# Hymba block on one core: state-space units on a closer pace, the mixing stage's start moved, Newton roots on GpSimd

## The chip, the cores and the metric

One core of one Trainium2 chip runs the whole layer in a single launch. The metric is the device time in microseconds, the median of three runs. Engines are named as in the profile: PE (TensorE) with its weight loads PEld, DVE (VectorE), ACT (ScalarE), POOL (GpSimd), and SP, whose queue issues most of the DMAs.

## The reference

A pre-normalised input (2048 tokens, width 1024) is projected once. Its columns feed a diagonal state-space layer (32 groups of 16 channels, 64 complex states each) and a chunked attention with 8 heads. Both outputs are normalised, joined, and projected back; then comes a SwiGLU feed-forward part and a last normalisation.

```python
h = rmsnorm(x, norm_mix_g)
proj = h @ w_in                       # u_ssm, q, k, v: 512 columns each
# state space: scan over time, y = Re(C s) + D u, then
y = gelu(y); y_ssm = y * sigmoid(y @ w_glu + b_glu)
y_att = chunked_attention(q, k, v, rel_bias)   # own chunk of 64 and 8 before
mixed = concat([rmsnorm(y_ssm, g_ssm), rmsnorm(y_att, g_att)])
x = x + mixed @ w_out
h2 = rmsnorm(x, norm_ffn_g)
x = x + (silu(h2 @ w_gate) * (h2 @ w_up)) @ w_down
out = rmsnorm(x, norm_final_g)
```

## The kernel before

Every large product is done in three matmuls of a reduced-precision float type: `split` makes a high part (a cast on ACT) and a low part (a subtraction on DVE), and `mm3` adds high x high, high x low and low x high. Tokens lie along the free dimension in four blocks of 512.

The stages follow each other:

- `u_phase` projects the state-space input and works out the state-space constants.
- `att_phase` runs attention in 128 steps (`scores`, then `transp` two steps later, then `pv_head` and `pv_scale`), one step for 128 queries of one head. Between the steps it advances units of other work: the projections of q, k and v (`qk_unit`, `v_unit`), the normalised inputs (`hT_unit`) and eight state-space units (`ssm_unit`). Each `Unit` has a first and a last step, and `advance` spreads its yields evenly over them. State-space unit b runs from step `2 + int(SW * b)` to `2 + int(SW * (b + 1))`.
- `mix_phase` is a generator too. At step `OPEN` = 119 the attention's input buffers are released and it is opened: it loads the gate's weights (`load_wg`, four tiles `sg` through two buffers). From step `GSTART` it is advanced to step 130: it loads the first block of state-space outputs (`load`: four DMAs into `yr`, one GELU into `ys`, splits into `gh` and `gl`) and of attention outputs (`load_a`), yields `PY` times, then runs the gate's matmuls (`glu`, 16 yields, with the norm's sums at yield `RA1` and the spread of its roots at `RA2`), and yields `PZ` times. The rest of the stage runs after the last step: the gate of the second block, `split_wo` for the eight tiles of `w_out`, then `w_out` block by block.
- `gate_up_phase` and `down_phase` are the feed-forward part.

A state-space unit loads its inputs through SP (`U`, `Bst`, `Tm`, `Vm`; `U` has one buffer), multiplies them (`pj<-U,Bst`), copies the result to `X` on ACT, scans it on POOL (L601 to L613), moves the states to `XG` by DMA (L635), forms the output (`pj<-U,Tm` and `pj<-XG,Vm`), and stores it (`y<-X`, L648).

`newton` turns a mean square into a reciprocal root: an integer seed, then three Newton steps, all on tiles of 128x4. It is called by `rstd1` in the mixing stage, by `rstd_steps` for the later norms, and by `u_phase`. `spread` then transposes the roots across partitions on PE.

The order of the instructions on an engine is the planner's: it orders by its own costs and by priority, except that PE's matmuls, and whatever else is passed to `keep_in_program_order`, keep the order of the program. DMAs of one queue are issued in order.

Of the kernel before, what the change touches and what calls it, by code (L numbers as in the profile page):

```python
# [11 lines left out]
I32 = mybir.dt.int32  # L12
AF = mybir.ActivationFunctionType
ALU = mybir.AluOpType
AX = mybir.AxisListType

P = 128
SEQ, D = 2048, 1024
KT = D // P
DS = 512  # L20
# [11 lines left out]
EPS = 1e-6  # L32
LAG = 2
NSMALL = 100
WB = 3
OPEN, GSTART = 119, 122
R1 = 13
SGB = 2
RA1, RA2 = 2, 12
# [7 lines left out]
LPH = 2  # L47
V0 = 0, 4
DB, XB = 3, 2
SW = 15  # L50
CUT = -8, -2, 2, 7, 13, 19, 24
CUTL = -8, -2, 2, 7, 13, 19, 23
ORDER = "sptf"
# [43 lines left out]
def f32(ap):  # L97
    return ap.bitcast(F32)


def newton(k, pool, ps, n, w):

    V = k.nc.vector
    v, f, y, o = (k.t(pool, t, [P, w], bufs=2) for t in ("nv", "nf", "ny", "no"))
    V.tensor_scalar(v[:], ps, 1.0 / n, EPS, op0=ALU.mult, op1=ALU.add)
    V.tensor_copy(f[:], v[:].bitcast(I32))
    V.tensor_scalar(f[:], f[:], -0.5, 1597463007.0, op0=ALU.mult, op1=ALU.add)
    V.tensor_copy(y[:].bitcast(I32), f[:])
    V.tensor_scalar(v[:], v[:], -0.5, None, op0=ALU.mult)
    for a, b in ((y, o), (o, y), (y, o)):  # L110
        V.tensor_tensor(f[:], a[:], a[:], op=ALU.mult)
        V.tensor_tensor(f[:], f[:], v[:], op=ALU.mult)
        V.scalar_tensor_tensor(b[:], f[:], 1.5, a[:], op0=ALU.add, op1=ALU.mult)
    return o


def tok_sums(k, te, ps, c, sq):

    for i in range(4):
        te.matmul(ps[:, c + i : c + i + 1], sq[:, i * P : (i + 1) * P], k.ones[:], start=True, stop=True)  # L120
# [5 lines left out]
        te.transpose(pb[:, i * P : (i + 1) * P], o[:, c + i : c + i + 1].to_broadcast([P, P]), k.ident[:])  # L126


def rstd_steps(k, te, psum, pool, tag, sq, n, out, **kw):

    nt = out.shape[-1] // P
    ps = k.t(psum, *tag, **kw)
    sqs = sq if isinstance(sq, list) else [sq]
    for i in range(nt):
        for m, sq in enumerate(sqs):
            te.matmul(ps[:, i : i + 1], sq[:, i * P : (i + 1) * P], k.ones[:], start=m == 0, stop=m == len(sqs) - 1)
    with k.tc.high_priority():
        o = newton(k, pool, ps[:, :nt], n, nt)
    yield
    pb = k.t(psum, *tag, **kw)  # L140
    for i in range(nt):
        te.transpose(pb[:, i * P : (i + 1) * P], o[:, i : i + 1].to_broadcast([P, P]), k.ident[:])
    k.nc.scalar.copy(out, pb[:, : nt * P])
    yield
# [8 lines left out]
def split(k, hi, lo, raw):  # L153
    nc = k.nc
    return nc.scalar.copy(hi, raw), nc.vector.tensor_tensor(lo, raw, f32(hi), op=ALU.subtract)  # L155
# [244 lines left out]
def u_phase(k, ident, S, aw):  # L400
# [3 lines left out]
    with ExitStack() as cx:  # L404
# [54 lines left out]
        def sums(b):  # L459
            with tc.high_priority():  # L460
                ST[b] = newton(k, p2 if b else aw, ST[b][:], D, 4)
# [215 lines left out]
def att_phase(k, ident, S, aw, x0, roots):  # L677

    tc, nc, io, pfs = k.tc, k.nc, k.io, k.pfs
    with ExitStack() as cx:  # L680
# [256 lines left out]
        for b in range(NG // GB):  # L937
            units.append(Unit(ssm_unit(k, sp, psum, S, b, k.ssm_eng), SSM_N, 2 + int(SW * b), 2 + int(SW * (b + 1)), light=SL))
        N = len(steps)
# [19 lines left out]
        yield mix  # L959


PY, PZ = 8, 1
MIX_N = 17 + PY + PZ


def mix_phase(k, S, bank):

    tc, nc, io = k.tc, k.nc, k.io
    te = k.te
    with ExitStack() as cx:  # L970
        rx = ExitStack()
        my = rx.enter_context(tc.tile_pool(name="my", reuse_waits="tile", bufs=1, side="right"))
        mz = rx.enter_context(tc.tile_pool(name="mz", reuse_waits="tile", bufs=1, side="right"))
# [5 lines left out]
        W, Wg = {}, {}  # L979
# [8 lines left out]
        def load_wo(n, pool, tag, **kw):  # L988
            raw = k.t(pool, tag, [P, 1024], **kw)
            nc.sync.dma_start(raw[:], io["w_out"][QS[n] * P : (QS[n] + 1) * P, :])  # L990
            return raw

        def split_wo(raws):
            for n, q in enumerate(QS):
                W[q] = k.t(mx, f"woh{q}", [P, D], F32R), k.t(mx, f"wol{q}", [P, D], F32R)
                raw = raws[n] if n < len(raws) else load_wo(n, wr, "xt")
                split(k, W[q][0][:], W[q][1][:], raw[:])

        def squares(src):
            sq = k.t(mz, "sq", [P, SB], bufs=2)  # L1000
# [14 lines left out]
        def load(sb, one=False):  # L1015
            b = B()
            b.o = {}
            yt = k.t(my, "ys", [P, 4, SB], bufs=2)
            b.ys, b.g = [yt[:, f] for f in range(4)], []
            if sb % 2 == 0:  # L1020
                yrs[0] = k.t(my, "yr", [P, 4, L, 128])
                for f in range(4):
                    nc.sync.dma_start(yrs[0][:, f], S["y"][f * P : (f + 1) * P, :, sb * 64 : sb * 64 + 128])
            yv = b.yr = yrs[0][:, :, :, (sb % 2) * 64 : (sb % 2 + 1) * 64]
            fs = [slice(0, 4)] if one else [slice(f, f + 1) for f in range(4)]
            for s in fs:
                nc.scalar.activation(yt[:, s].rearrange("p f (c j) -> p f c j", j=L), yv[:, s].rearrange("p f j c -> p f c j"), AF.Gelu_apprx_tanh)  # L1027
            for f in range(4):
                gh, gl = k.t(my, f"gh{f}", [P, SB], F32R), k.t(my, f"gl{f}", [P, SB], F32R)
                split(k, gh[:], gl[:], b.ys[f])  # L1030
                b.g.append((gh, gl))
            return b
# [33 lines left out]
        def rstd1(b, c, ps):  # L1066

            tok_sums(k, te, ps, 0, b.sqs if c else b.sqa)
            with tc.high_priority():
                b.o[c] = newton(k, mz, ps[:, :4], DS, 4)  # L1070

        def rstd2(b, c, pb):

# [3 lines left out]
        def big():  # L1077
            return k.t(psum, *BIG)

        def norm(b, n):  # L1080
            ps = big()
            pcs = [ps[:, 512 * c : 512 * c + 512] for c in range(2)]
            if n:
                for c in range(2):
                    spread(k, te, pcs[c], b.o[c], 0)
            for c in range(2):
                (rstd2 if n else rstd1)(b, c, pcs[c])
# [53 lines left out]
        b = load(0, True)  # L1141
# [4 lines left out]
        for n, _ in enumerate(glu(b, bank, True)):  # L1146
            if n == RA1:
                rstd1(b, 0, bank())
            if n == RA2:
                pb = bank()  # L1150
                spread(k, te, pb, b.o[0], 0)
                rstd2(b, 0, pb[:])
            yield
# [9 lines left out]
        for n, _ in enumerate(glu(nxt, bk, True)):  # L1163
            if n == R1:
                rstd1(b, 1, bk())
            yield
        psum, mx = k.psum, k.mx
        raws += [load_wo(n, mx, f"m{QS[n + 2]}") for n in range(2, 6)]
        b.m = {}
        mixed(b, 0)  # L1170
        split_wo(raws)
        load_a(nxt, 1)
        xr = pre = None
        for sb in range(NSB):
# [3 lines left out]
            if sb == 0:  # L1178
                held = [w_out(0, b, 2 * n) for n in range(2)]
                next(held[0])  # L1180
                ps = big()
# [27 lines left out]
            if sb < NSB - 1:  # L1209
                xr = rstd_steps(k, te, psum, k.mf, BIG, b.sa[:], D, S["rsn"][:, sb * SB : (sb + 1) * SB])  # L1210
# [3 lines left out]
            b = nxt  # L1214
# [121 lines left out]
def gate_up_phase(k, S):  # L1336
# [3 lines left out]
    with ExitStack() as cx:  # L1340
# [6 lines left out]
        def bank(n):  # L1347
            return k.t(psum[n], n, [P, 512])

        xr = rstd_steps(k, te, psum["X"], k.mf, ("X", [P, 512]), k.last, D, S["rsn"][:, (NSB - 1) * SB :])  # L1350

        raws = cycle((k.gr,) * 2 + (g2,) * 2)
# [121 lines left out]
def down_phase(k, S):  # L1474
    tc, nc, io = k.tc, k.nc, k.io
    V, te = nc.vector, k.te
    with ExitStack() as cx:
        fa = cx.enter_context(tc.tile_pool(name="fa", reuse_waits="tile", bufs=1))
        a0, r1, r2, a1 = (cx.enter_context(tc.tile_pool(name=n, reuse_waits="tile", bufs=b, side="right")) for n, b in (("a0", 1), ("r1", 4), ("r2", 6), ("a1", 1)))
        ring = cycle((r1,) * 4 + (r2,) * 6)  # L1480
        dx, dy = (cx.enter_context(tc.tile_pool(name=n, bufs=4, space=bass.MemoryType.PSUM, reuse_waits="tile")) for n in ("dx", "dy"))
# [50 lines left out]
        class End:  # L1532
# [15 lines left out]

            def sums(self):
                self.rs = k.t(fa, "rs", [P, 512])  # L1550
                self.r = rstd_steps(k, k.te, dy, fa, ("ps", [P, 512]), self.sa, D, self.rs[:, : self.n])
                next(self.r)

            def products(self):
# [144 lines left out]
```

## Time and profile before

| | us |
|---|---|
| median of 3 runs | 2292.94 (2292.49 to 2293.21) |
| the profiled execution's own time | 2291.46 |
| its span, first to last instruction | 2289.7 |
| PE busy | 2176.4 (95%) |
| DVE busy | 1544.3 (67%) |
| ACT busy | 1000.6 (44%) |
| POOL busy | 350.4 (15%) |

The mean granted clock of TensorE over the span is 0.976. Attention and the state-space units lie between about 125 and 740 us, the mixing stage's products end near 976, the gate and up products near 1820, and the down products run to the end. POOL works until about 683 us; behind that its row in the page is empty.

How the views are read: a row of the timeline gives the start, the duration, the engine, the line of the kernel, and the tiles written and read; in brackets stands how long the engine was idle before it and what ended that idle time. A row of SPq is the issue of a DMA. A row of the table of stretches gives a stretch's length and the busy time of PE, PEld, DVE, ACT and POOL in it (with instruction counts), the granted clock, the share of DMA time and the rate.

### The profile page before, as it was taken

How to read it: one execution, taken by the hardware profiler on the slowest of the kernel's cores; microseconds unless marked ns; L12 is line 12 of the kernel's file. 1: busy time of each engine (PE TensorE's matmuls, PEld its weight loads, DVE VectorE, ACT ScalarE, POOL GpSimd, SP SyncE). 2: the span in 40 equal slices, each digit the busy share in tenths (PEclk: the TensorE clock that was granted, in tenths of full speed). 3: DMA queues.
4: the chain of work that ended last, by engine and by line, in shares of the span. 5: the costliest groups of instructions: out<-in, count | busy, mean ns of one | idle time of the engine just before them, and what ended most of it. 6: DMA issues, size and time to landing. Idle time of an engine off the chain costs nothing.

```text
span 2289.7 us, 30275 instructions
## 1 busy us (share of the span) xinstructions
PE 2176.4 (95%) x10632; PEld 1833.7 (80%) x10632; DVE 1544.3 (67%) x2695; ACT 1000.6 (44%) x1655; POOL 350.4 (15%) x813
## 2 busy tenths in 40 slices
PE   8988899999997899999999999999999999999997
PEld 6777688898986688878888887888888778888886
DVE  7745565556556756776767678667666477688776
ACT  6444555455557552343333335333333343353321
POOL 2245765455660000000000000000000000000000
PEclk9998999999998899999999999999999999999998
DMA  8667786676643534854555467555333286465642
GB/s 299 229 224 221 257 219 205 188 199 172 191 133 116 170 124 153 274 180 143 180 179 202 160 204 266 186 173 198 129 97 111 99 326 240 167 231 181 221 161 74
DMA packets 215256, 428.33 MB, mean 187 GB/s; under 512 B 38592, under 2 KB 61168, under 8 KB 208000
## 3 DMA queue, kind: packets, MB, share of 16 engines
q1 hardware_dynamic: 210368, 412.50, 55.2%
q0 software_dynamic: 4736, 13.91, 2.0%
q8 instruction: 83, 1.36, 0.2%
q14 instruction: 69, 0.57, 0.1%
HBM read 286.86 MB, written 129.00 MB: 182 GB/s over the span
## 4 chain that ended last, share of the span: by engine, by line
PE 83%; DVE 4%; DMA 3%; issue 2%; ACT 2%; POOL 2%; SPq 1%; DVEq 0%; POOLq 0%; ACTq 0%
PE X L79 20%; PE ps L79 20%; PE Y L79 10%; PE pf L79 9%; PE big L79 9%; PE W L79 5%; PE pj L79 4%; PE sc L79 2%; PE pt L82 2%; SPq L563 1%; SPq L648 0%; POOL X L604 0%; DVE ptl L867 0%; ACT ys L1027 0%; DMA lo<-hc 0%
## 5 line engine op out<-in xcount | busy, mean ns | idle before, releaser
L79 PE MATMUL X<-hi,c 128*128 128x512 f32 x1408 | 451.2, 391 | 6.7 <-DVE c L155 5.4
L79 PE MATMUL ps<-hd,hd 128*128 128x512 f32 (+1 forms) x1968 | 432.9, 382 | 5.7 <-DVE hd L155 3.3
L79 PEld LDWEIGHTS ps<-hd,hd 128*128 128x128 f32 x1968 | 359.8, 190 | 77.4 <-DVE hd L155 4.4
L79 PEld LDWEIGHTS X<-hi,c 128*128 128x128 f32 x1408 | 265.6, 189 | 63.2 <-DVE c L155 6.3
L79 PE MATMUL X<-lo,c 128*128 128x512 f32 x704 | 275.1, 391 | 0.0
L155 ACT CAST hd<-hd 128x1536 fp32r<-128x1536 f32 (+1 forms) x106 | 147.6, 1393 | 238.0 <-DMA hd<-hq 189.0
L79 PE MATMUL Y<-hi,c 128*128 128x512 f32 x704 | 224.3, 389 | 1.5 <-DVE u L1388 1.5
L155 DVE TENSOR_TENSOR hd<-hd 128x1536 fp32r<-128x1536 f32 (+1 forms) x106 | 174.1, 1644 | 28.7 <-ACT hd L155 28.1
L155 DVE TENSOR_TENSOR c<-S,c 128x512 fp32r<-128x512 f32 x176 | 120.9, 688 | 97.0 <-ACT c L155 96.7
L1512 DVE TENSOR_TENSOR acc<-acc,ps 128x512 f32<-128x512 f32 x196 | 131.3, 684 | 52.3 <-PE ps L79 50.8
L1384 ACT COPY u<-X 128x512 f32<-128x512 f32 x132 | 77.4, 587 | 200.0 <-PE X L79 200.0
L79 PE MATMUL big<-m,woh 128*128 128x512 f32 x512 | 163.1, 400 | 0.0
L79 PE MATMUL pf<-hi,w 128*128 128x512 f32 x416 | 153.8, 422 | 8.5 <-ACT w L155 4.7
L155 ACT CAST c<-S 128x512 fp32r<-128x512 f32 x176 | 109.5, 622 | 119.3 <-PE Y L79 61.6
L79 PEld LDWEIGHTS Y<-hi,c 128*128 128x128 f32 x704 | 132.2, 188 | 29.7 <-DVE u L1388 2.2
L79 PEld LDWEIGHTS X<-lo,c 128*128 128x128 f32 x704 | 132.8, 189 | 27.7
L155 ACT CAST c<-raw 128x512 fp32r<-128x512 f32 x132 | 82.2, 623 | 151.9 <-PE Y L79 68.5
L79 PE MATMUL Y<-lo,c 128*128 128x512 f32 x352 | 137.0, 389 | 0.0
L867 DVE TENSOR_TENSOR ptl<-pt,pth 128x640 fp32r<-128x640 f32 (+3 forms) x152 | 98.3, 647 | 46.7 <-ACT pth L866 45.1
L851 ACT ACTIVATE s<-s,mn 128x640 f32<-128x640 f32 (+4 forms) x128 | 98.0, 765 | 65.4 <-DVE mn L848 60.7
L866 ACT CAST pth<-pt 128x640 fp32r<-128x640 f32 (+3 forms) x152 | 83.8, 551 | 92.0 <-PE pt L82 87.9
L79 PE MATMUL W<-hi,c 128*128 128x512 f32 x352 | 115.5, 389 | 0.0
(440 smaller groups left out, 4174.5 us busy)
## 6 DMA issues: line engine op xcount, KB each, us to landing
w<-wss SPq DMA_DIRECT2D x36, 1024.0 KB, 6.0
hq<-g SPq DMA_DIRECT2D x140, 256.0 KB, 2.1
hd<-hq SPq DMA_DIRECT2D x42, 768.0 KB, 4.5
hd<-wc SPq DMA_DIRECT2D x42, 768.0 KB, 6.0
raw<-in_w_gate SPq DMA_DIRECT2D x44, 512.0 KB, 3.7
raw<-in_w_up SPq DMA_DIRECT2D x44, 512.0 KB, 4.3
wc<-px SPq DMA_DIRECT2D x66, 256.0 KB, 3.2
wss<-w SPq DMA_DIRECT2D x12, 1024.0 KB, 5.6
```

The lines of the kernel that those rows point to most:

```text
L79: return self.tc.keep_in_program_order(self.tc.nc.tensor.matmul(*a, **b))
L82: return self.tc.keep_in_program_order(self.tc.nc.tensor.transpose(*a, **b))
L155: return nc.scalar.copy(hi, raw), nc.vector.tensor_tensor(lo, raw, f32(hi), op=ALU.subtract)
L563: ins = nc.sync.dma_start(out, in_)
L851: nc.scalar.activation(s[:, :nk], s[:, :nk], AF.Exp, bias=mn[:], scale=-1.0, accum_out=sums[sb, pr][:, hh, qp : qp + 1])
L866: nc.scalar.copy(pth[:, a:b, qp, :], pt[:, a:b, :])
L867: nc.vector.tensor_tensor(ptl[:, a:b, qp, :], pt[:, a:b, :], f32(pth[:, a:b, qp, :]), op=ALU.subtract)
L1384: nc.scalar.copy(u[:], ps[:])
L1512: V.tensor_tensor(a, a, ps[:], op=ALU.add)
```

## The change

- `SW` goes from 15 to 14.25: the eight state-space units start at steps 2, 16, 30, 44, 59, 73, 87 and 101 and the last ends at 116 (before: 2, 17, 32, 47, 62, 77, 92, 107, and 122).
- `GSTART` goes from 122 to 120 and `PY` from 8 to 11. `MIX_N` grows by three with it. The state-space buffers are released at step 120.
- `newton` makes its seed in one operation on integers in place of three. With `aside`, only the mean stays on DVE (kept in program order) and the remaining 14 operations go to POOL, where the fused third operation of a Newton step is two. `aside` holds for `rstd1` and for `rstd_steps` except at the tail; `u_phase` and the tail stay on DVE with 12 operations.
- The low halves of `split_wo` are kept in program order on DVE.

```diff
-OPEN, GSTART = 119, 122
+OPEN, GSTART = 119, 120
...
-SW = 15
+SW = 14.25
...
-def newton(k, pool, ps, n, w):
+def newton(k, pool, ps, n, w, aside=False):
 
-    V = k.nc.vector
+    V, E = k.nc.vector, k.nc.gpsimd if aside else k.nc.vector
     v, f, y, o = (k.t(pool, t, [P, w], bufs=2) for t in ("nv", "nf", "ny", "no"))
-    V.tensor_scalar(v[:], ps, 1.0 / n, EPS, op0=ALU.mult, op1=ALU.add)
-    V.tensor_copy(f[:], v[:].bitcast(I32))
-    V.tensor_scalar(f[:], f[:], -0.5, 1597463007.0, op0=ALU.mult, op1=ALU.add)
-    V.tensor_copy(y[:].bitcast(I32), f[:])
-    V.tensor_scalar(v[:], v[:], -0.5, None, op0=ALU.mult)
+    mean = V.tensor_scalar(v[:], ps, 1.0 / n, EPS, op0=ALU.mult, op1=ALU.add)
+    if aside:
+        k.tc.keep_in_program_order(mean)
+    E.tensor_scalar(y[:].bitcast(I32), v[:].bitcast(I32), -0.5, 1597463007.0, op0=ALU.mult, op1=ALU.add)
+    E.tensor_scalar(v[:], v[:], -0.5, None, op0=ALU.mult)
     for a, b in ((y, o), (o, y), (y, o)):
-        V.tensor_tensor(f[:], a[:], a[:], op=ALU.mult)
-        V.tensor_tensor(f[:], f[:], v[:], op=ALU.mult)
-        V.scalar_tensor_tensor(b[:], f[:], 1.5, a[:], op0=ALU.add, op1=ALU.mult)
+        E.tensor_tensor(f[:], a[:], a[:], op=ALU.mult)
+        E.tensor_tensor(f[:], f[:], v[:], op=ALU.mult)
+        if aside:
+            E.tensor_scalar(f[:], f[:], 1.5, None, op0=ALU.add)
+            E.tensor_tensor(b[:], f[:], a[:], op=ALU.mult)
+        else:
+            E.scalar_tensor_tensor(b[:], f[:], 1.5, a[:], op0=ALU.add, op1=ALU.mult)
     return o
...
-def rstd_steps(k, te, psum, pool, tag, sq, n, out, **kw):
+def rstd_steps(k, te, psum, pool, tag, sq, n, out, aside=True, **kw):
...
-        o = newton(k, pool, ps[:, :nt], n, nt)
+        o = newton(k, pool, ps[:, :nt], n, nt, aside)
...
-PY, PZ = 8, 1
+PY, PZ = 11, 1
...
-                split(k, W[q][0][:], W[q][1][:], raw[:])
+                k.tc.keep_in_program_order(split(k, W[q][0][:], W[q][1][:], raw[:])[1])
...
-                b.o[c] = newton(k, mz, ps[:, :4], DS, 4)
+                b.o[c] = newton(k, mz, ps[:, :4], DS, 4, True)
...
-                self.r = rstd_steps(k, k.te, dy, fa, ("ps", [P, 512]), self.sa, D, self.rs[:, : self.n])
+                self.r = rstd_steps(k, k.te, dy, fa, ("ps", [P, 512]), self.sa, D, self.rs[:, : self.n], False)
```

## The prediction

> **What bounds the kernel now.** I read the page first, then the table of stretches, then TensorE's timeline around the stretches where it is least busy, then the other engines' timelines there. The page, parts 1 and 2:
>
> ```profile
> PE 2176.4 (95%) x10632; PEld 1833.7 (80%) x10632; DVE 1544.3 (67%) x2695; ACT 1000.6 (44%) x1655; POOL 350.4 (15%) x813
> PEclk9998999999998899999999999999999999999998
> ```
>
> TensorE is busy 95% of the span, so its waits, and the stretches in which it is granted half its clock, are what a change of order can win or lose. The table of stretches (length, then busy time of PE, PEld, DVE, ACT, POOL, granted clock) says where they lie:
>
> ```profile
> 240.00:300.00 60.00, 48.26 (x273) 40.82 (x271) 35.68 (x83) 28.78 (x72) 33.30 (x76) 0.94 0.84 245
> 690.00:720.00 30.00, 18.06 (x89) 14.99 (x88) 14.68 (x33) 23.22 (x30) 0.00 (x0) 0.76 0.60 193
> 740.00:770.00 30.00, 22.03 (x92) 17.29 (x91) 29.38 (x53) 22.67 (x31) 0.00 (x0) 0.83 0.70 234
> 800.00:978.00 178.00, 175.43 (x808) 145.63 (x806) 119.09 (x257) 69.57 (x100) 0.00 (x0) 0.99 0.55 184
> ```
>
> The attention steps end and the mixing stage begins in 690 to 770; 12 and 8 us are idle there, and the clock falls to 0.76 and 0.83. From 800 TensorE has 2.6 us of idle in 178, so nothing done there for VectorE is worth more than that. In 240 to 300 it idles 11.7 us among the state-space units. TensorE's timeline names the two long waits (idle before an instruction stands in brackets):
>
> ```profile
> 681.42 0.39 PE L79 MATMUL pf<-hi,w 128*128 128x512 f32 x1
> 687.82 0.60 PE L79 MATMUL pj<-U,Tm 128*128 128x256 f32 x2
> 691.09 0.49 PE L79 MATMUL sc<-k,q2h 128*128 128x320 f32 x1
> 709.13 0.80 PE L79 MATMUL pf<-gh,wgh 128*128 128x512 f32 x1 [7.59 <-ACT gh L155]
> 711.30 0.63 PE L79 MATMUL pf<-gl,wgh 128*128 128x512 f32 x1
> 711.73 0.63 PE L79 MATMUL pf<-gh,wgl 128*128 128x512 f32 x1
> 739.38 0.39 PE L79 MATMUL big<-gl,wgh 128*128 128x512 f32 x1
> 739.61 0.39 PE L79 MATMUL big<-gh,wgl 128*128 128x512 f32 x1
> 756.83 0.39 PE L79 MATMUL big<-m,wol 128*128 128x512 f32 x1
> 765.13 1.09 PE L82 MATMUL big<-ident,no 128*128 128x128 f32 x4 [7.91 <-DVE no L113]
> ```
>
> The last projection of attention is issued at 681.42; the gate's first matmul waits 7.59 us for the GELU's split; the spread of the norm's roots waits 7.91 us for the Newton chain. Matmuls of 512 columns follow each other every 0.23 us at full clock (739.38, 739.61) and every 0.43 just after the first wait (711.30, 711.73): the clock is halved after a long wait, here until about 715, so 6 us do 3.2 us of work and 2.8 are lost. After 765 it lasts some 4.6 us and costs 2.3.
>
> **The gate's start.** What the GELU waited for, by the queue of SP and ScalarE's timeline:
>
> ```profile
> 687.78 0.33 SPq L985 DMA_DIRECT2D sg<-in_w_glu  x1
> 689.51 0.52 SPq L1023 DMA_DIRECT2D yr<-y  x1
> 692.09 3.62 SPq L648 DMA_DIRECT2D y<-X  x8
> 698.21 0.34 SPq L901 DMA_DIRECT2D ya_s<-ya  x1
> 698.78 0.53 SPq L1023 DMA_DIRECT2D yr<-y  x1
> 703.12 1.28 ACT L1027 ACT_TABLE_LOAD   x1 [0.85 <-DMA yr<-y]
> 704.41 3.64 ACT L1027 ACTIVATE ys<-yr 128x2048 f32<-128x2048 f32 x1
> ```
>
> The fourth load of `yr` stands behind the stores of the last state-space unit and a store of `ya`, and is issued at 698.78. In the changed order (read from the built programs) the last unit's eight stores stand ahead of attention's last `q2h` loads, because the units end at step 116 and not at 122, and the fourth `yr` stands right behind the fourth `sg`, as the third does here at 689.51. The `sg` loads still wait for VectorE's `wgl` splits (two buffers), and those now stand one score step later; score steps follow each other by 2.16 us here:
>
> ```profile
> 685.51 0.82 DVE L848 CUSTOM_DVE_ANT_0 s<-sc,nba 128x640 f32<-128x640 f32 x1
> 687.67 0.82 DVE L848 CUSTOM_DVE_ANT_0 s<-sc,nba 128x640 f32<-128x640 f32 x1
> ```
>
> So the fourth `yr` is issued near 691.5, 7.3 us sooner after the last projection, and with it the GELU and the gate. Against that stand the last unit's output matmuls (687.82 to 691.09, 3.3 us), which now precede that projection and were no filler for the wait, and one step's scores and transposes, 1.1 us, that now follow the gate's first matmul. 7.3 - 3.3 - 1.1 = **2.9 us gained**, bounds 0 (the queue is late for another reason, such as the third `sg`) and 7.3. The wait itself shrinks to some 5 us, so I take half of the clock's 2.8 as won: **1.4** (0 to 2.8). Eleven yields in place of eight ahead of the gate put its start at step 123 instead of 124; the load moves from step 122 to 120. Nothing waits in the two steps between that does not wait before: their cover is attention's own scores.
>
> **The roots on POOL.** The chain that held the spread, on VectorE:
>
> ```profile
> 753.85 0.15 DVE L105 TENSOR_SCALAR nv<-big 128x4 f32<-128x4 f32 x1
> 753.92 1.22 DVE L155 TENSOR_TENSOR wol<-m,woh 128x1024 fp32r<-128x1024 f32 x1
> 764.83 0.16 DVE L113 SCALAR_TENSOR_TENSOR no<-nf,ny 128x4 f32<-128x4 f32 x1
> ```
>
> From the mean at 753.85 to the root at 764.99 it takes 11.1 us, although its 14 operations are 0.16 us each: one long operation stands between any two. In the changed order the mean keeps its place on VectorE (pinned, like the `wol` splits), and 14 operations of 128x4 go to POOL, which is idle. What they cost there depends on what VectorE does meanwhile:
>
> ```profile
> 129.13 0.20 POOL L286 TENSOR_TENSOR cp<-a 128x16 f32<-128x16 f32 x1
> 129.72 1.09 POOL L283 TENSOR_TENSOR cp<-a 128x16 f32<-128x16 f32 x1
> 129.47 1.25 DVE L155 TENSOR_TENSOR w<-raw,w 128x1024 fp32r<-128x1024 f32 x1
> ```
>
> The same operation takes 0.20 us alone and 1.09 beside a VectorE split of two SBUF operands: it ends when that ends. Alone the chain is 14 x 0.20, some 3 us. Behind the mean the changed order has on VectorE four `wol` splits (1.14 apart), one PSUM read and two `ys` products, then the products that need the spread: about 6.4 us in which POOL gets one operation per long one and a few beside the PSUM read, some eight; the other six run free in 1.3. So 7.5 us in place of 11.1, **3.6 gained** at the spread, bounds 7.6 (POOL free, 0.3 us of the wait left) and -4 (each of 14 behind a 1.09: 15 us, which the seven operations there don't supply). Half of the clock's 2.3 goes with it: **1.2**. [...] The later pairs of roots have some 13 us until their spread and VectorE idles there: nothing. The two operations fewer per root elsewhere, on VectorE, are worth 0.16 each where the tail waits for them: **0.3**. The pinned `wol` splits keep the place they had.
>
> **The units paced by 14.25 steps.** This moves every load, POOL scan and output of units 1 to 7 against attention. Each unit's scan runs on POOL while TensorE works on; TensorE's waits at the units:
>
> ```profile
> 213.27 0.67 PE L79 MATMUL pj<-XG,Vm 128*128 128x256 f32 x2 [1.25 <-DMA nbb<-nbs]
> 282.03 0.67 PE L79 MATMUL pj<-XG,Vm 128*128 128x256 f32 x2 [1.61 <-DMA XG<-X]
> 349.95 0.59 PE L79 MATMUL pj<-XG,Vm 128*128 128x256 f32 x2
> PE pj L79 <- DMA Tm<-kts: 8.2, 3, 3.5
> PE pj L79 <- DMA U<-u: 2.6, 1, 2.6
> ```
>
> The first three units have no slack at their output; the other five wait for nothing there. Pricing the matmuls between a unit's input and output by 0.23 us per 512 columns, in both orders, the cover of the eight changes by -2.5, -3.9, -3.0, -0.4, -0.2, -4.3, -2.7 and +3.8 us. The scan does not get faster, so the first three could wait up to 9.4 us more in all. Below that: in 240 to 300 TensorE also waits for ScalarE and VectorE, and work that reaches them with more lead waits less; I take a third, **3.0 lost** (0 to 9.4). The waits for the next unit's loads (8.2 + 2.6 above) come where `U` loads stand behind `y` stores in SP's queue; in the changed order units 2 and 7 lose such neighbours, units 5 and 6 gain them: **0.5 lost** (-3 to +5). Longer waits cost clock too: **1.0** (0 to 4.5).
>
> **Sum.** -2.9 - 1.4 - 3.6 - 1.2 - 0.3 + 3.0 + 0.5 + 1.0 = -4.9. The profiled execution took 2291.46 us (span 2289.7); the median of the runs, 2292.94, is 1.5 above it, so the same step gives **2288.0** for the median. A measurement of this kernel tells 0.2%, 4.6 us, from no change.
>
> **Rivals.** *Output before scan* (slower): TensorE reaches the outputs of units 0 to 2 ahead of POOL's scans, all 9.4 us are waited, and three waits of over 3 us each lose 1.5 of clock: 9.4 + 4.5 + 0.5 - 9.4 (the gains) = +5.0, 2297.9. For it: the rows at 213.27 and 282.03; against it: it holds only if none of the neighbouring waits gives way. It decides once the pacing costs over 9.4 us.
> *The mixing stage starts no sooner* (no change): the `yr` loads are late behind the third and fourth `sg`, so the gate's 2.9 + 1.4 don't come: -0.6, 2292.3. For it: `wgl` stands later; against: the stores that held the queue are gone.
> *POOL unhindered and pacing free*: the spread's wait falls by 7.6, its clock's 2.3 and the gate's 2.8 come whole, nothing is lost at the units: -2.9 - 2.8 - 7.6 - 2.3 - 0.3 = -15.9, 2277.0. Against it: the two-operand splits behind the mean.
>
> **Chances.** The forecast 0.40 (its own range 2283 to 2291), POOL unhindered 0.22, no sooner 0.18, output before scan 0.20. Of the forecast's share 0.28 lies under 2288.3. So faster 0.50, same 0.12 + 0.18 = 0.30, slower 0.20. The range reaches from 2276 to 2299, past both outer cases' own values by about 1 us.
>
> **What would show it.** Right: the gate's first matmul some 20 us after the last projection (27.7 here), a wait of 3 to 5 us before the spread, POOL operations of 128x4 near 0.2 us or as long as the split beside them, the waits at `XG` of units 0 to 2 longer by a few us. Wrong: a wait before the gate of 7 us again, the spread waiting as long for POOL as for VectorE, or over 9 us more waiting at the units.

## The result and the profile after

The changed kernel takes 2349.73 us (median; 2347.32 to 2354.98) against 2293.07 for the kernel before on the same chip: ratio 1.0247, 95% interval 1.0225 to 1.0269. That is 57 us slower; the forecast was 2288.0, its range 2276 to 2299. The profiled execution of the changed kernel has a span of 2345.9 us, 56.2 more than before.

The page of the changed kernel, part 1:

```profile
PE 2193.1 (93%) x10632; PEld 1846.4 (79%) x10632; DVE 1527.6 (65%) x2521; ACT 1001.0 (43%) x1655; POOL 390.6 (17%) x981
```

TensorE issues the same 10632 matmuls and is busy 16.7 us longer. That part follows the granted clock, 0.976 over the span before and 0.965 now. The rest of the 56.2, 39.5 us, is idle time (span less busy: 113.3 before, 152.8 after). Every run below is split in this way.

Where it lies, by the table of stretches, cut at the same five events in both kernels: the end of the last projection, the gate's first matmul, the first spread, the first product of the feed-forward part. (Length, then busy time of PE, PEld, DVE, ACT and POOL, granted clock, DMA share, GB/s.) First the kernel before:

```profile
100.00:681.80 581.80, 534.67 (x3206) 477.27 (x3206) 334.36 (x621) 302.52 (x647) 320.76 (x755) 0.96 0.68 203
681.80:709.10 27.30, 14.45 (x91) 12.32 (x89) 14.65 (x27) 20.76 (x33) 1.21 (x2) 0.87 0.78 243
709.10:765.10 56.00, 46.15 (x213) 36.98 (x214) 46.73 (x93) 39.70 (x52) 0.00 (x0) 0.87 0.31 108
765.10:975.30 210.20, 209.41 (x952) 174.20 (x953) 135.41 (x304) 84.80 (x120) 0.00 (x0) 0.97 0.52 172
975.30:2289.70 1314.40, 1283.38 (x5733) 1063.54 (x5731) 935.75 (x1384) 497.54 (x718) 0.00 (x0) 0.99 0.53 179
```

The changed kernel:

```profile
100.00:709.50 609.50, 545.51 (x3222) 484.24 (x3221) 334.39 (x621) 303.99 (x649) 318.84 (x757) 0.94 0.66 195
709.50:731.60 22.10, 10.23 (x67) 8.23 (x65) 13.11 (x25) 18.30 (x28) 0.00 (x0) 0.85 0.70 222
731.60:787.80 56.20, 45.81 (x222) 37.30 (x222) 42.25 (x64) 39.32 (x51) 10.52 (x28) 0.93 0.33 119
787.80:1031.50 243.70, 218.34 (x952) 181.26 (x953) 128.88 (x194) 87.13 (x124) 27.20 (x126) 0.91 0.45 149
1031.50:2345.90 1314.40, 1283.36 (x5733) 1064.04 (x5731) 932.08 (x1359) 496.94 (x717) 5.68 (x14) 0.99 0.53 178
```

Two stretches carry the loss: attention with the state-space units (+27.7) and the products of the mixing stage (+33.5). The way to the gate is 5.2 shorter, the gate's own stretch is unchanged, and so is everything behind the mixing stage. TensorE's timeline at the points that the prediction named, and at new ones:

```profile
213.26 1.19 PE L79 MATMUL pj<-XG,Vm 128*128 128x256 f32 x2 [5.17 <-DMA XG<-X]
285.19 1.19 PE L79 MATMUL pj<-XG,Vm 128*128 128x256 f32 x2 [8.82 <-DMA XG<-X]
807.22 0.95 PE L79 MATMUL big<-ones,sq 128*128 128x1 f32 x8
814.18 1.87 PE L79 MATMUL big<-ones,sq 128*128 128x1 f32 x8 [6.01 <-DVE nv L105]
1007.11 1.11 PE L82 MATMUL big<-ident,no 128*128 128x128 f32 x4 [6.86 <-POOL no L115]
```

The waits of the last two rows are new, and two more like that at 814 follow, 5.5 and 7.0 us long. The sums of a block's first norm are done by 808; those of the second, in another half of the same PSUM tile, wait 6 us for VectorE's `nv`, the mean over the first. Why the mean is late, by VectorE's and ScalarE's timelines:

```profile
810.30 2.28 DVE L1011 TENSOR_TENSOR sq<-sq,sg 128x512 f32<-128x512 f32 x3
812.63 0.69 DVE L1121 TENSOR_TENSOR sa<-sa,xt 128x512 f32<-128x512 f32 x1
813.36 0.69 DVE L1122 TENSOR_TENSOR sa<-sa,xt 128x512 f32<-128x512 f32 x1
813.97 0.15 DVE L105 TENSOR_SCALAR nv<-big 128x4 f32<-128x4 f32 x1
811.56 1.04 ACT L1120 ACTIVATE xt<-xt 128x1024 f32<-128x1024 f32 x1
```

VectorE first adds the squares of the next block and of the output rows; these precede the mean in the program, and the last ones wait for ScalarE's square at 811.56. In the kernel before the mean was not kept in order, had high priority, and went ahead of them: its second sums waited 0.25 us. VectorE's and TensorE's timelines of the kernel before at the same point (the squares of the next block follow at 786.75):

```profile
785.30 0.16 DVE L105 TENSOR_SCALAR nv<-big 128x4 f32<-128x4 f32 x1 [0.86 <-PE big L79]
785.52 1.05 PE L79 MATMUL big<-ones,sq 128*128 128x1 f32 x8 [0.25 <-DVE nv L105]
```

### The profile page after: what moved, and what is told of

It is laid out like the page before. It is cut to its first block, busy times and chain, and to the rows that moved or that the text cites. A ratio compares the mean times of both kernels' runs of the same rounds, so it can differ in the third digit from the quotient of the medians.

```text
span 2345.9 us, 30295 instructions
## 1 busy us (share of the span) xinstructions
PE 2193.1 (93%) x10632; PEld 1846.4 (79%) x10632; DVE 1527.6 (65%) x2521; ACT 1001.0 (43%) x1655; POOL 390.6 (17%) x981
## 4 chain that ended last, share of the span: by engine, by line
PE 80%; DVE 5%; DMA 4%; POOL 4%; issue 3%; ACT 2%; SPq 1%; DVEq 0%; POOLq 0%; ACTq 0%
PE X L79 20%; PE ps L79 20%; PE Y L79 10%; PE pf L79 9%; PE big L79 8%; PE W L79 5%; PE pj L79 4%; PE sc L79 2%; PE pt L82 2%; SPq L567 1%; DMA xt<-in_xp 1%; POOL X L608 1%; POOL X L607 1%; DMA lo<-hc 1%; POOL st L606 1%
## 5 line engine op out<-in xcount | busy, mean ns | idle before, releaser
L1516 DVE TENSOR_TENSOR acc<-acc,ps 128x512 f32<-128x512 f32 x196 | 131.4, 684 | 54.5 <-PE ps L79 52.4
L855 ACT ACTIVATE s<-s,mn 128x640 f32<-128x640 f32 (+4 forms) x128 | 97.9, 765 | 69.3 <-DVE mn L852 64.6
L79 PEld LDWEIGHTS big<-m,woh 128*128 128x128 f32 x512 | 100.9, 199 | 21.4 <-issue 0.3
```

The lines of the kernel that those rows point to most:

```text
L79: return self.tc.keep_in_program_order(self.tc.nc.tensor.matmul(*a, **b))
L855: nc.scalar.activation(s[:, :nk], s[:, :nk], AF.Exp, bias=mn[:], scale=-1.0, accum_out=sums[sb, pr][:, hh, qp : qp + 1])
L1516: V.tensor_tensor(a, a, ps[:], op=ALU.add)
```

## The experiments

Theory A: there are two separate losses, the closer pace and the fixed place of the mean on VectorE. Its rivals (B: the roots on POOL; C: the earlier start disturbs the units' loads; D: the start costs more than it brings; G: the late roots themselves) and, for the pace, theory E (the units are a chain with a pace of its own) against F (single waits, by chance of alignment) stand in the expectations. Differences in us below are of the median to that of the kernel before on the same chip (the ratio is formed from the runs themselves and can differ from them by a few us); idle time and TensorE's busy time are from the profiled execution. A run has 4 to 12 executions, pace1350 only two.

| run | median | before, same chip | ratio (95%) | PE busy | idle |
|---|---|---|---|---|---|
| kernel before | 2292.94 | | 1 | 2176.4 | 113.3 |
| changed | 2349.73 | 2293.07 | 1.0247 (1.0225 to 1.0269) | 2193.1 | 152.8 |
| pin_dve | 2325.49 | 2293.55 | 1.0138 (1.0123 to 1.0153) | 2184.9 | 137.0 |
| nopin | 2327.64 | 2293.55 | 1.0151 (1.0135 to 1.0167) | 2192.1 | 139.3 |
| sums_first | 2323.85 | 2295.10 | 1.0128 (1.0101 to 1.0156) | 2186.3 | 135.0 |
| roots_nopin | 2301.29 | 2297.44 | 1.0018 (1.0002 to 1.0035) | 2177.3 | 124.4 |
| pace | 2310.57 | 2293.55 | 1.0085 (1.0059 to 1.0110) | 2174.4 | 134.5 |
| pace1350 | 2340.61 | 2297.44 | 1.0183 (1.0162 to 1.0203) | 2195.3 | 144.3 |
| pace_ypool | 2312.75 | 2297.44 | 1.0058 (1.0042 to 1.0073) | 2187.4 | 123.9 |
| ypool | 2290.69 | 2297.44 | 0.9965 (0.9950 to 0.9980) | 2174.9 | 108.6 |
| pacestart | 2321.02 | 2293.55 | 1.0123 (1.0106 to 1.0140) | 2186.3 | 132.5 |
| pace_gs | 2320.71 | 2295.10 | 1.0105 (1.0080 to 1.0130) | 2187.5 | 131.4 |
| first | 2287.87 | 2295.10 | 0.9966 (0.9952 to 0.9979) | 2171.7 | 114.8 |
| ypseed | 2288.82 | 2295.10 | 0.9965 (0.9952 to 0.9978) | 2180.8 | 107.7 |

### The mean's fixed place

**pin_dve**, from the kernel before: the seed in one operation, all roots on VectorE, the mean and the low halves kept in order.

```diff
+    if aside:
+        k.tc.keep_in_program_order(mean)
...
-                split(k, W[q][0][:], W[q][1][:], raw[:])
+                k.tc.keep_in_program_order(split(k, W[q][0][:], W[q][1][:], raw[:])[1])
```

> The kernel before with the one-operation seed, all roots on VectorE, and the mean and the low halves of w_out kept in program order there; pacing and start as before. Theory A: the fixed place alone makes the second sums wait some 5 to 7 us three times and costs 20 to 35 us: 2313 to 2328. Rival B: within 4 us of the kernel before, 2289 to 2297.

Measured: 1.0138, +32 us, with all roots on VectorE. Waits of TensorE from 765 us to the feed-forward part (us in all, times, longest), the row of the means:

```profile
PE big L79 <- DVE nv L105: 18.6, 3, 7.0
```

VectorE's timeline at the first of them:

```profile
789.58 0.69 DVE L1118 TENSOR_TENSOR sa<-sa,xt 128x512 f32<-128x512 f32 x1 [1.42 <-ACT xt L1117]
790.30 0.69 DVE L1119 TENSOR_TENSOR sa<-sa,xt 128x512 f32<-128x512 f32 x1
790.91 0.15 DVE L105 TENSOR_SCALAR nv<-big 128x4 f32<-128x4 f32 x1
```

It is the changed kernel's picture without POOL: same place, same waits (18.5 us, 3 times there). The last spread waits 6.97 us for its root on VectorE here and 6.86 for POOL's in the changed kernel, so that wait too comes from the late mean and not from POOL. Rival B falls. That the mean and not the low halves is to blame follows from the next run, in which these keep their place.

**nopin**, from the changed kernel:

```diff
-    if aside:
-        k.tc.keep_in_program_order(mean)
```

> The changed kernel without the fixed place of the mean on VectorE; the rest of the chain stays on POOL, the low halves of w_out keep their fixed place. Theory A: the three waits of 5 to 7 us before the second sums of each block (814, 881 and 951 us) and the one of 6.9 us before the last spread (1007) go, with the half clock behind them, about 30 us: 2316 to 2322. Rival B (the roots on POOL are what holds the mixing stage): 2343 to 2352, with the waits still there.

Measured: 1.0151, +34 us, 23 less than the changed kernel's 57. The waits behind the first spread (itself 5.7 us, for POOL) and up to the feed-forward part:

```profile
PE X L79 <- ACT c L157: 3.4, 1, 3.4
PE big L79 <- DVE nv L105: 1.3, 3, 0.6
```

The three waits for the mean are gone (1.3 us are left), and the stretch takes 214.7 us in place of 243.7. The median lies 6 us above what theory A gave: a wait of 3.4 us stands before the first product of the feed-forward part, and the profiled execution, itself 6 us above the run's median, took 8.2 us longer in the attention part than the changed kernel's (617.8 and 609.5): 3.4 us more idle time, the rest TensorE's longer time for the same matmuls.

**sums_first**, from the changed kernel, pin and POOL kept:

```diff
-            for c in range(2):
-                (rstd2 if n else rstd1)(b, c, pcs[c])
+            if not n:
+                for c in range(2):
+                    tok_sums(k, te, pcs[c], 0, b.sqs if c else b.sqa)
+            for c in range(2):
+                rstd2(b, c, pcs[c]) if n else rstd1(b, c, pcs[c], False)
...
-            tok_sums(k, te, ps, 0, b.sqs if c else b.sqa)
+            if sums:
+                tok_sums(k, te, ps, 0, b.sqs if c else b.sqa)
```

> The changed kernel with one reordering: in the mixing stage the token sums of both norms of a block are issued on TensorE one after the other, and then both means; the means keep their fixed place on VectorE. Theory A (the late mean costs because the second sums share a PSUM tile with the first and stand behind its read, with all of TensorE's queue behind them): the three waits of 5.5 to 7 us at 814, 881 and 951 us go with their half clock, only the one ahead of the last spread (6.9 us) stays: 2322 to 2332. Rival G (the late roots themselves are what is waited for, and the wait moves on to the spread): 2342 to 2352.

Measured: 1.0128, +29 us, 28 less than the changed kernel, as theory A has it. Waits from 792 us to the feed-forward part:

```profile
PE big L82 <- POOL no L115: 11.5, 3, 5.6
```

No wait for a mean is left, although the means are as late as before: the cost came through the shared PSUM tile, on which TensorE's second sums stood, with all its products behind them. Of rival G only a little is true: two later spreads wait 2.95 and 2.97 us for their roots (theory A had let the last one stay at 6.9).

**roots_nopin**, from the kernel before: the roots on POOL, the seed, the low halves kept in order, but not the mean.

> The kernel before, its pacing and start, with the roots behind the mean on POOL, the one-operation seed and the fixed order of w_out's low halves, but without the fixed place of the mean. If POOL's chain is worth what the trace of the changed kernel shows at the first spread (7.9 us of wait down to 5.6) and costs nothing later: 2288 to 2292. If it holds the last root ahead of the feed-forward part (a wait of 3 us there and three stretches of half clock, as in the run without the fixed place): 2295 to 2301.

Measured: 1.0018, +4 us, as the second expectation has it. The first spread waits 5.6 us as expected, but the later end loses what that wins: idle time from the first spread to the feed-forward part is 6.9 us in place of 0.8. POOL's chain was no gain for this kernel even without the pin.

### The closer pace

**pace**, from the kernel before:

```diff
-SW = 15
+SW = 14.25
```

> The kernel before with the state-space units paced by 14.25 steps and nothing else. Theory A (two separate losses: the pacing before the last projection, the mean's fixed place on VectorE behind it): in the changed kernel the last projection of attention comes 27.7 us later than before, with 3.3 us of output matmuls moved ahead of it, so the pacing alone gives +20 to +28 us, 2313 to 2321, with waits at XG of about 5 and 9 us near 213 and 285 us. Rival C (the earlier opening of the mixing stage disturbs the units' loads, the pacing is nearly free): within 5 us of the kernel before, 2288 to 2298.

Measured: 1.0085, +17 us, just below theory A's +20 to +28; the span is 19.2 longer, and idle time alone is 21.2 more. The attention part is 27.1 us longer (608.9), as in the changed kernel; 8.3 of it come back between there and the feed-forward part. Of these, 5.6 lie behind the gate's start and are nearly all less TensorE time for the same matmuls (granted clock 0.92 and 0.98 in the two stretches there, 0.87 and 0.97 in the kernel before). Waits of TensorE from 100 to 710 us:

```profile
PE pj L79 <- DMA Tm<-kts: 15.2, 4, 7.9
PE pj L79 <- DMA XG<-X: 14.2, 2, 8.9
```

`Tm<-kts` stands for the waits at a unit's input, whose loads are issued together with these, `XG<-X` for those at its output. So the pacing alone brings the waits of the changed kernel (15.8 and 14.0 us there), without the earlier start: rival C falls. Why it costs so much, by one unit of this run (timelines of PE, POOL and SP):

```profile
224.57 1.97 PE L79 MATMUL pj<-U,Bst 128*128 128x256 f32 x8 [1.94 <-DMA Tm<-kts]
228.82 0.51 POOL L601 TENSOR_TENSOR st<-X,a 128x128 f32<-128x128 f32 x1 [23.63 <-ACT X L587]
273.86 1.21 POOL L635 DMA_DIRECT2D XG<-X  x2 [0.30 <-POOL X L613]
281.39 1.19 PE L79 MATMUL pj<-XG,Vm 128*128 128x256 f32 x2 [8.92 <-DMA XG<-X]
286.79 3.60 SPq L648 DMA_DIRECT2D y<-X  x8
290.49 3.82 SPq L563 DMA_DIRECT2D U<-u  x8
643.40 1.89 PE L79 MATMUL pj<-U,Bst 128*128 128x256 f32 x8
692.24 0.59 PE L79 MATMUL pj<-XG,Vm 128*128 128x256 f32 x2
```

Everything in a link waits for what stands before it: the input at 224.6, 46 us of scan on POOL, 6 us until the states are there, the output, then stores and loads in SP's queue, and the next input at 298. The eighth unit's input comes at 643.4 and the first came at 156.5: 69.6 us for each link. In the kernel before it is (639.7 - 159.4) / 7 = 68.6. The closer pace does not make the chain faster. TensorE merely reaches each link sooner and waits, and the attention steps that had covered the waits come behind the last unit, where only they are left.

**pace1350**: the same with `SW = 13.5`.

> The kernel before with the units paced by 13.5 steps (the last ends at step 110, twelve before the last of the kernel before; with 14.25 it is six). Theory E: the last unit's output stands at 692 to 699 us as with 14.25 steps (692) and with 15 (688), since the chain is no faster, and six more steps of attention come behind it: 2330 to 2340, the last projection some 25 us later again. Rival F: the waits grow in proportion to the lost cover, the last unit's output moves forward by 10 us or more, and the time is 2300 to 2320.

Measured: 1.0183, 2340.61 us, +43. TensorE's timeline, first and eighth input, and the last unit's output:

```profile
156.35 1.89 PE L79 MATMUL pj<-U,Bst 128*128 128x256 f32 x8
638.18 2.71 PE L79 MATMUL pj<-U,Bst 128*128 128x256 f32 x8 [2.10 <-DMA U<-u]
686.08 0.67 PE L79 MATMUL pj<-XG,Vm 128*128 128x256 f32 x2 [3.12 <-DMA XG<-X]
```

A link takes 68.8 us again, and the last output stands at 686, where it was 688 with a pace of 15 and 692 with 14.25. Twelve steps fewer to run them in brought the units 2 us forward; the last projection ends at 729.5 (681.8 before, 708.9 with 14.25). Theory E had said 2330 to 2340, which the time meets but for 0.6, and 692 to 699 for the output, which comes earlier; rival F, with 10 us or more for the output and 2300 to 2320, falls.

**pace_ypool** and **ypool**: the units' output stores on POOL's queue, with the pace of 14.25 and of 15.

```diff
-                nc.sync.dma_start(S["y"][b * F : (b + 1) * F, j, :]...
+                eng.dma_start(S["y"][b * F : (b + 1) * F, j, :]...
```

> The pacing of 14.25 steps alone, with the eight stores of each unit's output issued from POOL's queue and not SP's. Theory E (the units are a chain that sets its own pace: 42 to 50 us of scan on POOL, 6 us until the states have moved, 3 us of output, 11 to 14 us of stores and loads in SP's queue, about 68 us for each; a closer pace only pushes attention's work behind the chain): the next loads no longer stand behind 3.2 us of stores, so each of the seven links gets up to 3.2 us shorter, and 10 to 20 of the 17 us that the pacing cost come back: 2291 to 2301. Rival F (single waits by chance of alignment): 2306 to 2315.

> The kernel before with the output stores of the units on POOL's queue. Theory E: the pace of 15 steps is close to that of the chain, waits of some 11 us at the next unit's first matmuls shrink to a few: 2283 to 2290. Rival F: 2290 to 2297.

Measured: 0.9965 for ypool, 7 us faster than the kernel before by the medians and 8 by the ratio, and 1.0058 for pace_ypool, 2 or 6 us better than the pace alone (medians, ratios) where theory E had 10 to 20. Timelines of SP and POOL at one unit of ypool:

```profile
421.73 4.81 SPq L563 DMA_DIRECT2D U<-u  x8
422.98 4.04 POOL L648 DMA_DIRECT2D y<-X  x8 [13.75 <-ACT X L645]
```

The loads no longer stand behind the stores, and POOL was idle. A link takes 67.8 us (158.4 to 633.3), and with the pace of 14.25 67.6 (157.3 to 630.9). So theory E holds for the direction, and its size was wrong: a link won 0.8 and 2.0 us, not 3.2. Links of the same pace differ from trace to trace, but the groups do not overlap: with the stores on SP's queue they take 68.5 to 69.9 us at a pace of 15 (three traces) and 69.3 to 70.2 at 14.25 (six), with the stores on POOL's 67.6 to 68.2 (four). The waits for loads at the units' inputs fall from 10.8 to 4.6 us in ypool, as theory E had it. By their bare times both runs lie in rival F's ranges; but the kernel before, 2293 when these were set, took 2297.4 on the chip of these runs. Of the 12.5 us that pace_ypool won in the attention part against pace (596.4 and 608.9) at most half reached the end: over the whole span TensorE idles 10.6 us less than in pace, but takes 13.0 us longer for the same matmuls, nearly all of it behind the gate's start.

### The earlier start

**pacestart**, and **pace_gs** with `PY` left at 8:

```diff
-OPEN, GSTART = 119, 122
+OPEN, GSTART = 119, 120
...
-PY, PZ = 8, 1
+PY, PZ = 11, 1
```

> The pacing of 14.25 steps and the earlier start (gate load at step 120, eleven yields), roots as before. Theory A: the gate's first matmul follows the last projection 22 us later in place of 27.7, so the pacing alone less 0 to 5 us, 2311 to 2319; the mixing stage behind 800 us runs as in the kernel before (2 to 3 us of idle TensorE up to the feed-forward part). Rival C: here and not under the pacing alone stands the loss of some 23 us. Rival D (the start costs more than it brings): over 3 us above the pacing alone.

> The pacing of 14.25 steps with the mixing stage loaded from step 120 on, but with eight yields ahead of the gate as before (eleven in the change). With the eleven the run stood 10 us above the pacing alone, with 2 us less of idle TensorE and 11 us more lost to half clock. Theory H (the start costs by where its waits fall for the clock, not by waits): idle time within 3 us of the pacing alone, and a time anywhere between 2306 and 2322 that follows the half-clock stretches. Rival D (the early load holds up ScalarE's and SP's queues, and so attention's last steps): 4 us or more of additional idle time between the last projection and the spread, 2316 to 2324.

Measured: 1.0123 and 1.0105, by the medians 10 and 9 us slower than the pace alone, by the ratios 9 and 5, with intervals that overlap that of the pace alone. The profiled executions have 2.0 and 3.1 us less idle time than it and 12 to 13 us more TensorE time for the same matmuls. Theory A's 2311 to 2319 for pacestart is missed by 2 us. The stretches of pacestart up to the first spread:

```profile
709.20:731.80 22.60, 11.64 (x65) 9.49 (x64) 13.08 (x24) 18.28 (x28) 0.00 (x0) 0.76 0.70 222
731.80:791.80 60.00, 47.76 (x222) 38.75 (x223) 48.29 (x96) 41.32 (x55) 0.00 (x0) 0.87 0.32 114
```

And of pace:

```profile
708.90:733.50 24.60, 12.21 (x75) 9.70 (x73) 13.91 (x26) 19.17 (x30) 0.00 (x0) 0.82 0.72 227
733.50:786.40 52.90, 43.41 (x214) 35.15 (x214) 47.26 (x94) 40.42 (x53) 0.00 (x0) 0.92 0.34 119
```

The gate does start 2 us sooner behind the last projection, at a lower clock (0.76 and 0.87 against 0.82 and 0.92). Theory H fits both: the idle time changes little and the time follows the clock. The time that rival D gave came too, but not its mechanism: idle time from the last projection to the spread is 1.3 and 0.2 us more than in pace, not 4. Whether the start draws these half-clock stretches or merely met them was not separated, and three things speak for chance in part. Of the 10.0 us by which pace_gs's span is longer than pace's, 6.0 are there already at the eighth unit's input (649.4 and 643.4 us), before anything of the earlier start. From the gate to the feed-forward part pacestart takes 270.1 us, 9.5 more than pace but only 3.9 more than the kernel before. And one of the four executions of the pace alone took 2322.4 us at a mean clock of 0.969, the others 2310.0 to 2310.8 at 0.973 to 0.976.

### A faster version

**first**: ypool with the one-operation seed, and POOL for the root ahead of the first spread alone. **ypseed**: ypool with the seed alone.

```diff
-                b.o[c] = newton(k, mz, ps[:, :4], DS, 4)
+                b.o[c] = newton(k, mz, ps[:, :4], DS, 4, aside)
...
-                rstd1(b, 1, bk())
+                rstd1(b, 1, bk(), True)
```

> The kernel before with the units' output stores on POOL's queue, the one-operation seed, and POOL for one root alone, the one ahead of the first spread; nothing is kept in program order that was not before. If the gains add: 8 us from the stores (measured), 2 to 3 from the spread's wait (7.9 to 5.6) with up to 2 of clock: 0.993 to 0.996 of the kernel before. If POOL's chain brings nothing there: as with the stores alone, 0.9965.

> The kernel before with the units' output stores on POOL's queue and the one-operation seed, all roots on VectorE. Two operations fewer among the long ones ahead of the first spread: the wait there (8.3 us with the stores alone) falls to 6 to 7.5; 0.994 to 0.9965 of the kernel before. If the seed brings nothing: 0.9965.

Measured: 0.9966 and 0.9965. Both beat the kernel before, by 0.35%, and the changed one, and neither differs from ypool: what they gain comes from the stores. The spread's wait falls, to 6.2 and 6.8 us from 8.3, but not the time; a gain of 2 us is within the intervals, and idle and clock elsewhere vary by more.

## Why the prediction was wrong, point by point

By the medians the parts come to 17 us for the pace (pace), 10 for the earlier start (pacestart less pace), 23 for the mean's fixed place (the changed kernel less nopin) and 4 for the roots on POOL with the seed and the order of the low halves (roots_nopin): 54 of the 57, each uncertain by a few us.

- **The pinned mean** is the step that failed worst. The prediction looked only at the first spread, where the mean "keeps its place", and put the later roots at nothing because they have "some 13 us until their spread". It checked who waits for the roots and not who waits for the mean. TensorE's next sums do, and the pin held the mean behind sums for which ScalarE was late. Priced at 0; nopin and sums_first put it at 23 and 28 us, pin_dve at 32 with the seed and the low halves. The row of the kernel before that would have told (785.52: a wait of 0.25 us for `nv` before the second sums) does not stand in the prediction.
- **The pacing**, priced at +4.5, cost 17 (pace). The term was worked out per unit, as cover lost against a fixed scan, bounded by 9.4; "output before scan" was the right rival in direction. What failed is the picture of eight separate waits. The units are one chain of some 68 us a link, and what counts is when its last link ends (688, 692 and 686 us for paces of 15, 14.25 and 13.5) and how much attention is left behind that. The waits at the units grew from 13.6 us (8.2 + 2.6 + 1.6 + 1.2) to 29.8 (15.8 + 14.0), those at the inputs by 5.0, the upper bound given, those at the outputs by 11.2, past the 9.4.
- **The gate's start.** The queue moved as said; SP's row of the fourth load in the changed kernel:

```profile
719.63 0.52 SPq L1027 DMA_DIRECT2D yr<-y  x1
```

  The fourth `yr` is issued 10.1 us after the last projection's end, 17.0 before: 6.9 sooner, where 7.3 were forecast. The gate follows that end by 22.1 us in place of 27.3, 5.2 sooner, but with less beside it: the wait is 7.30 us (7.59 before), where 5 was expected, and idle time in this stretch fell by 1.0. So the 2.9 was 1.0 at most, and the clock's 1.4 did not come; in its place pacestart and pace_gs take 9 to 10 us more than pace by the medians, with less idle time and more clock lost, and how much of that the start itself causes stays open.
- **POOL's chain at the first spread** was near: the wait fell from 7.91 to 5.58 us, 2.3 in place of 3.6. The chain, by POOL's and VectorE's timelines:

```profile
778.84 0.17 DVE L105 TENSOR_SCALAR nv<-big 128x4 f32<-128x4 f32 x1
780.70 1.23 DVE L159 TENSOR_TENSOR wol<-m,woh 128x1024 fp32r<-128x1024 f32 x1
781.83 2.36 DVE L159 TENSOR_TENSOR wol<-xt,woh 128x1024 fp32r<-128x1024 f32 x2
779.09 1.10 POOL L108 TENSOR_SCALAR ny<-nv 128x4 int32<-128x4 int32 x1 [32.49 <-DVE nv L105]
780.74 3.52 POOL L112 TENSOR_TENSOR nf<-nf,nv 128x4 f32<-128x4 f32 x1
787.55 0.20 POOL L115 TENSOR_TENSOR no<-nf,ny 128x4 f32<-128x4 f32 x1
```

  It takes 8.9 us from the mean to the root, not 7.5. The 0.20 us that the prediction called "alone" (129.13) stood beside a VectorE operation on `xt<-pf,rsn` (128.18 to 129.55), one of whose inputs lies in PSUM; the last operations here, with VectorE idle, take the same 0.20. One operation of 128x4 lasted 3.52 us beside three splits that followed each other without a gap; the prediction had one operation per split. Beside a VectorE operation that reads PSUM (`yr<-big,bg`, 780.04 to 780.79) two others took 0.23 and 0.20 us (780.27 and 780.46).
- **The tail** (0.3) cannot be seen: the stretch behind the mixing stage takes 1314.40 us in both.
- Of the signs named in advance, two of the three that were to show it wrong appeared: a wait of 7 us before the gate, and over 9 us more at the units. The wait that cost most was on neither list.

## What to carry to other kernels

Before an operation is kept in program order, ask who reads or overwrites what it frees, not only who waits for its result: a 0.15 us read of PSUM can hold the whole TensorE queue (6.01 us at 814 in the changed kernel) if the planner's priority had been carrying it ahead of other work. Units that hand one buffer on from link to link have a pace of their own (67.6 to 70.2 us a link here); measure the time per link first, and pace no closer than that, since work pulled forward from beside a chain is work that later runs beside nothing. If the chain is to end sooner, take something out of a link, as the stores were taken out of SP's queue here.

## What the runs showed of the hardware

The clock weighed as much as some of the edits: for the same 10632 matmuls TensorE was busy between 2171.7 us (first) and 2195.3 (pace1350), and twice the profiled execution with less idle time was the slower one (pacestart against pace, ypseed against first). Whether the short pause before the second sums (0.25 us) is followed by half clock goes with where it falls. In pace the second sums of two blocks wait 0.26 us at 805.9 and 0.25 us at 923.8, with the same one-column matmuls on both sides of the wait and the same products behind them. The stretches of 3.4 us in which these waits lie, and those behind them (the table of stretches; the granted clock is the number behind POOL's):

```profile
803.20:806.60 3.40, 3.15 (x22) 2.79 (x21) 1.60 (x3) 1.26 (x2) 0.00 (x0) 1.00 0.12 30
806.70:810.10 3.40, 3.40 (x17) 2.84 (x17) 3.38 (x20) 0.63 (x1) 0.00 (x0) 1.00 0.83 293
922.70:926.10 3.40, 3.15 (x23) 2.85 (x22) 2.93 (x12) 0.58 (x1) 0.00 (x0) 1.00 0.41 154
926.10:929.50 3.40, 3.40 (x10) 2.61 (x9) 3.40 (x17) 1.06 (x1) 0.00 (x0) 0.50 0.65 240
```

After the first the clock stays full, after the second it is halved for 3.4 us, which get through 10 matmuls in place of 17. The half-clock stretches of a trace begin and end at multiples of 3.41 us from each other (in pace 782.8, 789.6, 926.1, 929.5; in the kernel before 759.9, 770.2, 787.2, 790.7, 906.7, 910.1). Counted on from them, such steps of 3.41 us divide the trace into windows. The 2.25 us of one-column matmuls and waiting lie, but for 0.1 us, within one window at 923 (922.7 to 926.1), and run over the end of one at 806 (806.7). What stands ahead is not the same: at 923 it is a spread of four 128-column matmuls, at 806 products. But pace's remaining block, with a spread ahead as at 923, has its sums from 863.7 to 865.9, over a window's end at 864.7, and keeps full clock.

The same holds in the eleven traces in which the second sums wait 0.25 to 1.3 us (all but the changed kernel, pin_dve and sums_first). Of their 33 blocks, the 20 whose sums lie within one window, to about 0.1 us, are followed by half clock; the 13 whose sums run over a window's end by a quarter of a us or more are not. The kernel before has both: its sums from 784.3 to 786.6 and from 903.8 to 906.1 lie within the windows that end at 787.2 and 906.7, where 3.41 us of half clock begin; those from 844.9 to 847.2 run over the end at 845.3, and the clock stays full. No run moved the sums on purpose, so this is read off the traces and was not tried. In the window from 922.7 to 926.1 us of pace 0.25 us of idle time, with one-column matmuls beside it, was enough.

A POOL operation of 128x4 that takes 0.20 us with VectorE idle (787.55 in the changed kernel) took 3.52 beside three back-to-back VectorE splits (780.74), longer than any single one of them (1.23).
